# A two-layer decoder trunk on one core: the pooling's channel maps multiplied into the projection's columns on the chip, and a new order of all instructions

## The chip, the core and the metric

The kernel runs on one core of a Trainium2 chip. A core has five engines that each work through a queue of their own in order: TensorE (PE in the profile; matrix products, and PEld for the loading of their stationary operand), VectorE (DVE), ScalarE (ACT), GpSimd (POOL) and SyncE (SP), which issues every DMA of this kernel. Engines wait for each other by semaphores. Data lie in SBUF (128 partitions), matrix products end in PSUM, inputs and stores lie in HBM. The metric is device time of one execution in microseconds (us): 1537.63 us is the median of three runs of the kernel before (1532.89 to 1539.34).

## The reference, cut to what matters

One sequence of 2048 tokens with 1024 channels passes a hybrid layer, a convolution layer and a last RMSNorm, all in float32. The change touches the first projection and the pooling behind it:

```python
def _even_mixer(h, w_in, pool_w, pool_scale, ...):
    proj = jnp.einsum('bsd,de->bse', h, w_in)          # 1024 -> 2048
    u_pool = proj[..., :POOL_WIDTH]                    # 512 channels: 4 groups of 128
    u_ssm = proj[..., POOL_WIDTH:MIX_WIDTH]
    z = proj[..., MIX_WIDTH:]
    y_pool = _multiscale_pool(u_pool, pool_w, pool_scale)
    y_ssm = _s5(u_ssm, ...)                            # diagonal state space model, then a GLU
    y = jnp.concatenate([y_pool, y_ssm], axis=-1) * jax.nn.silu(z)
    return jnp.einsum('bse,ed->bsd', y, w_out)

def _multiscale_pool(u, pool_w, pool_scale):
    ...
    for g, w in enumerate(POOL_WINDOWS):               # windows 2, 4, 8, 16
        c = csum[:, :, g, :]
        lag = jnp.pad(c, ((0, 0), (w, 0), (0, 0)))[:, :s, :]
        outs.append((c - lag) / jnp.minimum(pos, float(w)) - u32[:, :, g, :])
    pooled = jnp.stack(outs, axis=2)
    mixed = jnp.einsum('bsgc,gcd->bsgd', pooled, pool_w)       # one 128x128 map per group
    return mixed.reshape(b, s, POOL_WIDTH) * pool_scale
```

The window mean less the token works along the tokens, channel by channel; the map `pool_w` works along the channels. The second layer is a projection to 3072 columns, a causal convolution over 31 tokens for each of 1024 channels, a LayerNorm, gates and an output projection.

## The kernel before, in words

The tokens are handled as two halves of 1024 (h = 0 and 1, called A and B), each with two blocks of 512 (b). A matrix product of the model is done as three products of rounded operands: every weight and every activation is split by ACT and DVE into a rounded part "hi" (ACT, a CAST, L322) and a rest "lo" (DVE, a subtraction, L290), and `hi*hi + hi*lo + lo*hi` is summed in PSUM (`proj_ops`, products of 128x512, L351). A *unit* is one weight tile of 128 columns against 1024 tokens: 8 x 3 x 2 = 48 such products. For half A the first layer's units stand in the order s0 to s3 (state space columns), then pu0, pz0, pu1, pz1, ... pz3 (pooled columns and their gates), then z0 to z3. The first three units of a half, and the last three of half A, are done block by block, so that three units are open at once. Then come the same units of half B, the output products of A, the second layer of A and so on, at last the output products A.q and B.q.

Everything beside these units is written as small Python generators ("threads") with priorities. `Sched` puts all of it into one order when the program is built: it keeps a clock for each engine, gives each instruction a duration from a formula (in `tt`, `act`, `dma`, `mmb` and others), and takes the instruction that could start first, with a tolerance and the priorities. So the formulas set the order that each engine's queue has on the chip, and nothing else.

Memory is handed out in slots: `mm`, three PSUM tiles of 1024 columns, one for each open unit; `aux`, two PSUM tiles of 512; `raw` (2) for weights as loaded, `w` (8) for their hi and lo; `st` (8), `po` (2), `act` (25) for the rest. `fetch_thread` loads the weights in the units' order, `split_thread` splits them.

The pooling of a half and a group is `pool_thread`: load the projected group (`upd`), add it to shifted copies of itself, subtract the token, load `pool_w`, split both, multiply them in six products into an `mm` tile, load the gate (`z0d`), and multiply PSUM, gate and `pool_scale` on DVE (L308). `x_rates` computes the RMSNorm's factors of a half from eight loads of x; it writes them to HBM with 128x8 single numbers (`rsd`) and loads them back to all partitions. The first evacuation of a unit multiplies by them, so it needs that load. `ssm_prep` and what it spawns compute the tables of the state space model on DVE, ACT and PE and move them by DMA (`Kd`, `Wd`, `Md`).

Of the kernel before, what the change touches and what calls it, by code (L numbers as in the profile page):

```python
# [73 lines left out]
class Sched:  # L74
# [3 lines left out]
    EPS = SLACK  # L78

# [58 lines left out]

    def emit(self, op):
        start = max(self.clk[op.eng], op.ready)  # L140
        if op.eng == "SP":
            issue = start + 0.66
            self.clk["SP"] = issue
            self.dma = max(self.dma, issue) + op.dur
            end = self.dma + 1.9
        else:
            end = start + op.dur
            self.clk[op.eng] = end
# [58 lines left out]

    def run(self):
        while self.threads:
# [13 lines left out]
            est = lambda t: max(self.clk[t.op.eng], t.op.ready)  # L223
            first = min(cand, key=est)
            e0 = est(first)
            eng = first.op.eng
            near = [t for t in cand if t.op.eng == eng and est(t) <= e0 + self.EPS[eng]]
            th = min(near, key=lambda t: (t.bulk, t.prio, est(t)))
# [6 lines left out]
def trunk(ctx, tc, io):  # L235
# [24 lines left out]
    slots("pwt", 1, 256)  # L260
# [24 lines left out]

    def tt(o, a, b, op, eng=None):
        if eng is G:
            return Op("G", 0.25 + width(o) * 2.1e-3, [a, b], [o], lambda: G.tensor_tensor(o, a, b, op))  # L288
        d = 0.13 + width(o) / 960.0 + (0.13 if isps(a, b) else 0.0)
        return Op("V", d, [a, b], [o], lambda: V.tensor_tensor(o, a, b, op))  # L290

    def ts(o, a, s1, s2=None, op0=ALU.mult, op1=None, eng=None):
# [8 lines left out]
        if eng is G:  # L301
            return Op("G", 0.25 + width(o) * 1e-3, rd, [o], emit)
        return Op("V", 0.15 + width(o) / (960.0 if isps(a) else 1920.0), rd, [o], emit)

    def stt(o, a, s, b, op0, op1):
        rd = [a, b] + ([s] if isinstance(s, bass.AP) else [])
        d = 0.13 + width(o) / 960.0 + (0.13 if isps(a, b) else 0.0)
        return Op("V", d, rd, [o], lambda: V.scalar_tensor_tensor(o, a, s, b, op0, op1))  # L308

    def vcopy(o, a):  # L310
        return Op("V", 0.13 + width(o) / 960.0, [a], [o], lambda: V.tensor_copy(o, a))

    def recip(o, a):
        return Op("V", 0.13 + width(o) / 120.0, [a], [o], lambda: V.reciprocal(o, a))

    def scan(o, r, x, ini):
        rd = [r, x] + ([ini] if isinstance(ini, bass.AP) else [])
        return Op("V", 0.13 + width(o) / 480.0, rd, [o], lambda: V.tensor_tensor_scan(
            o, r.to_broadcast([128, width(o)]), x, ini, ALU.mult, ALU.add))

    def acopy(o, a):
        return Op("A", 0.05 + width(o) / 960.0, [a], [o], lambda: A.copy(o, a))  # L322

    def amul(o, a, m):
        return Op("A", 0.1 + width(o) / 960.0, [a], [o], lambda: A.mul(o, a, m))

    def act(o, a, fn, **kw):
# [5 lines left out]
        return Op("A", (0.3 if len(wr) > 1 else 0.13) + width(o) / 960.0, rd, wr, lambda: A.activation(o, a, fn, **kw))  # L333

    def gset(o, v):
        return Op("G", 0.25 + width(o) * 0.5e-3, [], [o], lambda: G.memset(o, v))

    def dma(o, i):
        n = int(np.prod(o.shape)) * 4
        run = 4 * min(a.ap[-1][1] if a.ap[-1][0] == 1 else 1 for a in (o, i))  # L340
        slow = 1.0 if run >= 512 else 1.5 if run >= 256 else 2.0
        return Op("SP", slow * n / 360e3, [i], [o], lambda: SP.dma_start(out=o, in_=i))

    def mmb(batch):

        d = sum(width(o) / 2400.0 if x.dtype == F32R else max(width(o), 128 if w.shape[1] > 64 else 0) / 600.0
                for o, w, x, s, e in batch) + 0.0027 * len(batch)
# [14 lines left out]
    def trb(batch):  # L362
# [3 lines left out]
        op = Op("PE", 0.11 * len(batch), [b[1] for b in batch] + [batch[0][2]], [b[0] for b in batch], emit)  # L366
# [49 lines left out]
    rsd = [dram(f"rsd{h}", (8, 128)) for h in range(2)]  # L416
    Ed = [dram(f"Ed{u}", (128, 1024)) for u in range(8)]
# [11 lines left out]
    class Job:  # L429
        def __init__(self, src, name):  # L430
            self.src, self.name, self.pool = src, name, "w"
# [4 lines left out]
    def job_cols(w, c0, name):  # L436
        return Job(w[c0 // 128], name)

# [76 lines left out]
    def rsqrt_of(o, a, n):  # L515
        t = yield Alloc("sml")
        tv = t[:, :n]
        yield Op("G", 0.3, [a], [o], lambda: G.tensor_tensor(o, a, mhalf[:, :n], ALU.pow))  # L518
# [182 lines left out]

    def pool_worker(h):
# [4 lines left out]
    def pool_thread(h, gi):  # L707
# [16 lines left out]
        if h == 0:  # L724
# [20 lines left out]
        free("st", hi_, lo_)  # L745
        free("pwt", w2)
# [3 lines left out]
        free("st", s)  # L750
# [1055 lines left out]
```

## Time and profile before

| | |
|---|---|
| median of three runs | 1537.63 us |
| the profiled execution | 1537.14 us, its span 1535.3 us |
| mean granted TensorE clock | 0.991 |
| PE busy | 1481.3 us, 96% |
| DVE, ACT, POOL busy | 1128.9, 524.2, 103.6 us |
| DMA | 280.77 MB, mean 183 GB/s |

The profiled execution lies 0.49 us under the median; about 1.8 us of it lie outside the span. PE is busy nearly throughout, so the time is PE's work and the places where PE stands. Busy time of an engine is the union of its instructions: the mean of one product of 128x512 is 397 ns, but they overlap, and one starts every 0.229 us. A product of unrounded float32 operands stands in the trace as two records.

### The profile page before, as it was taken

The numbers are of one execution on the slowest core, as the hardware profiler recorded it, in microseconds if no ns is written. First come the engines' busy times: TensorE is split into PE (matmuls) and PEld (weight loads), VectorE is DVE, ScalarE is ACT, GpSimd is POOL, SyncE is SP. The second block draws the span as 40 slices with busy tenths as digits, with TensorE's granted clock in tenths as the row PEclk, the third lists the DMA queues.
The fourth block names the chain that finished last, engine by engine and source line by source line (L and its number), as shares of the span: only waits on it lengthen the run. The fifth ranks groups of instructions, "written<-read, shape, count | busy, mean of one in ns | idle before, by whom it ended". The sixth has DMA issues, their size and how long they took to land. (4 is left out here: it accounts for less than half of the span.)

```text
span 1535.3 us, 18361 instructions
## 1 busy us (share of the span) xinstructions
PE 1481.3 (96%) x6942; PEld 1213.6 (79%) x6942; DVE 1128.9 (74%) x1318; ACT 524.2 (34%) x829; POOL 103.6 (7%) x313
## 2 busy tenths in 40 slices
PE   5899979999999999999999999999999999999997
PEld 3678768788888888888888888888888888887785
DVE  7882648887877533399999999245997898967652
ACT  6113433122135225311111530352364465443431
POOL 1000010110000002000000000120000000003322
PEclk9999989999999999999999999999999999999999
DMA  8238966877775763223253442623476485956743
GB/s 302 96 97 235 331 193 216 266 239 263 239 252 191 207 229 124 83 83 110 82 111 122 179 164 97 220 83 111 98 177 204 133 284 172 363 206 222 257 158 116
DMA packets 165464, 280.77 MB, mean 183 GB/s; under 512 B 55712, under 2 KB 86144, under 8 KB 165376
## 3 DMA queue, kind: packets, MB, share of 16 engines
q1 hardware_dynamic: 165376, 279.61, 56.1%
q8 instruction: 54, 0.88, 0.2%
q14 instruction: 34, 0.28, 0.1%
HBM read 183.93 MB, written 91.43 MB: 179 GB/s over the span
## 5 line engine op out<-in xcount | busy, mean ns | idle before, releaser
L351 PE MATMUL mm<-act,w 128*128 128x512 f32 x4224 | 1002.3, 397 | 29.0 <-ACT w L322 11.1
L351 PEld LDWEIGHTS mm<-act,w 128*128 128x128 f32 x4224 | 793.1, 189 | 211.8 <-ACT w L322 11.1
L308 DVE SCALAR_TENSOR_TENSOR ca<-cg,cwt,ca 128x1024 f32<-128x1024 f32 (+1 forms) x360 | 397.8, 1106 | 14.5 <-ACT ca L333 4.2
L351 PE MATMUL mm<-w,act 128*128 128x512 f32 x1344 | 318.9, 397 | 1.4 <-DVE w L290 1.4
L351 PEld LDWEIGHTS mm<-w,act 128*128 128x128 f32 x1344 | 253.3, 189 | 60.8 <-DVE w L290 1.9
L322 ACT CAST w<-raw 128x1024 fp32r<-128x1024 f32 (+1 forms) x117 | 121.3, 1038 | 265.8 <-PE mm L351 207.2
L290 DVE TENSOR_TENSOR w<-raw,w 128x1024 fp32r<-128x1024 f32 (+1 forms) x117 | 141.6, 1212 | 51.4 <-ACT w L322 50.1
L333 ACT ACTIVATE junk<-st 128x1024 bf16<-128x1024 f32 (+1 forms) x64 | 54.0, 844 | 135.1 <-DVE st L290 122.3
L290 DVE TENSOR_TENSOR po<-mm,st 128x1024 f32<-128x1024 f32 x32 | 46.6, 1455 | 70.6 <-PE mm L351 65.6
L290 DVE TENSOR_TENSOR st<-st,mm 128x512 f32<-128x512 f32 x48 | 30.9, 684 | 76.0 <-PE mm L351 76.0
L322 ACT COPY st<-aux 128x512 f32<-128x512 f32 (+2 forms) x56 | 25.7, 471 | 129.5 <-PE aux L351 100.8
L322 ACT CAST act<-st 128x512 fp32r<-128x512 f32 (+1 forms) x64 | 51.8, 853 | 46.7 <-DVE st L308 16.6
L333 ACT ACTIVATE act<-act,mask 128x128 f32<-128x128 f32 x192 | 57.8, 390 | 18.8 <-DMA act<-band 18.8
L290 DVE TENSOR_TENSOR act<-st,act 128x512 fp32r<-128x512 f32 (+1 forms) x64 | 56.3, 920 | 3.5 <-ACT act L322 3.3
L308 DVE SCALAR_TENSOR_TENSOR st<-st,mm 128x1024 f32<-128x1024 f32 x24 | 34.4, 1432 | 25.8 <-PE mm L351 25.8
L333 ACT ACTIVATE st<-mm 128x1024 f32<-128x1024 f32 x24 | 24.6, 1026 | 83.2 <-PE mm L351 81.0
L308 DVE SCALAR_TENSOR_TENSOR act<-aux,vcol,act 128x512 fp32r<-128x512 f32 x32 | 22.5, 746 | 40.3 <-ACT act L333 40.3
L518 POOL TENSOR_TENSOR sml<-sml,mhalf 128x1 f32<-128x1 f32 (+2 forms) x38 | 28.0, 736 | 346.5 <-DVE sml L298 343.7
L290 DVE TENSOR_TENSOR st<-st 128x512 f32<-128x512 f32 (+4 forms) x44 | 41.2, 937 | 9.8 <-DMA st<-upd 8.4
L351 PEld LDWEIGHTS aux<-st,act 128*128 128x128 f32 x384 | 45.5, 192 | 2.9 <-ACT act L333 1.4
L351 PE MATMUL aux<-st,act 128*128 128x128 f32 (+1 forms) x384 | 45.5, 274 | 1.1 <-ACT act L333 1.0
L351 PE MATMUL mm<-act,act 128*128 128x512 f32 x192 | 44.9, 393 | 0.8 <-DVE st L290 0.8
(144 smaller groups left out, 937.7 us busy)
## 6 DMA issues: line engine op xcount, KB each, us to landing
raw<-in_odd_w_in SPq DMA_DIRECT2D x48, 512.0 KB, 3.7
raw<-in_even_w_in SPq DMA_DIRECT2D x31, 512.0 KB, 5.1
st<-x1d SPq DMA_DIRECT2D x48, 256.0 KB, 4.9
st<-in_xT SPq DMA_DIRECT2D x16, 512.0 KB, 6.0
st<-in_x SPq DMA_DIRECT2D x16, 512.0 KB, 9.0
raw<-in_even_w_out SPq DMA_DIRECT2D x16, 512.0 KB, 3.7
z1d<-po SPq DMA_DIRECT2D x16, 512.0 KB, 3.2
st<-z1d SPq DMA_DIRECT2D x16, 512.0 KB, 6.2
```

The lines of the kernel that those rows point to most:

```text
L290: return Op("V", d, [a, b], [o], lambda: V.tensor_tensor(o, a, b, op))
L308: return Op("V", d, rd, [o], lambda: V.scalar_tensor_tensor(o, a, s, b, op0, op1))
L322: return Op("A", 0.05 + width(o) / 960.0, [a], [o], lambda: A.copy(o, a))
L333: return Op("A", (0.3 if len(wr) > 1 else 0.13) + width(o) / 960.0, rd, wr, lambda: A.activation(o, a, fn, **kw))
L351: nc.tensor.matmul(o, w, x, start=s, stop=e)
L518: yield Op("G", 0.3, [a], [o], lambda: G.tensor_tensor(o, a, mhalf[:, :n], ALU.pow))
```

## The change

Two things are changed together.

The first is the map of the pooling. The window mean less the token and the channel map can be exchanged, so the map is multiplied into the 512 pooled columns of `even_w_in` instead of onto the pooled sums. The new thread `pool_fold` does it on the chip, once for each of the four groups: it loads the group's columns in a new layout (`pool_in`, with the output channels on the partitions) and the map, multiplies them in 8 float32 products of 128x128 (two times 4 into an `aux` tile), copies the results by ACT and stores them in HBM (`wpd`). The units pu0 to pu3 of both halves load their weights from there (`job_fold`). In `pool_thread` the map's load, the splits of map and sums, the six products and their `mm` tile are gone; the last step multiplies the sums, the gate and `pool_scale` from SBUF.

The second is the order. The formulas for durations are replaced: `dma` now has a duration, an issue time and a landing time by the size of runs, with 8.7 ns for each run under 64 bytes; strided operands, ScalarE's and GpSimd's forms and float32 products have other times; an engine's own earlier write now counts as something to wait for (PE excepted). The whole program is ordered anew by them.

```diff
+    OVER = {"PE": 0.0, "V": 0.084, "A": 0.1, "G": 0.0}
...
-                    if a < hi and lo < b and p0 < q1 and q0 < p1 and (wr or w) and (e != op.eng or e == "SP"):
-                        r = max(r, t + 0.1)
+                    if a < hi and lo < b and p0 < q1 and q0 < p1 and (wr or w) and not (e == op.eng == "PE"):
+                        r = max(r, t + 0.05)
...
         if op.eng == "SP":
-            issue = start + 0.66
-            self.clk["SP"] = issue
-            self.dma = max(self.dma, issue) + op.dur
-            end = self.dma + 1.9
+            dur, issue, land = op.dur
+            self.clk["SP"] = start + issue
+            self.dma = max(self.dma, start + 0.5) + dur
+            end = self.dma + land
...
-        slow = 1.0 if run >= 512 else 1.5 if run >= 256 else 2.0
-        return Op("SP", slow * n / 360e3, [i], [o], lambda: SP.dma_start(out=o, in_=i))
+        rows = n // max(run, 4)
+        if run >= 1024:
+            d = n / 408e3
...
+        else:
+            d = rows * 8.7e-3
...
+    def job_fold(gi, name):
+        return Job(wpd[gi], name, ("wp", gi))
...
+            yield Wait(job.key)
...
+    def pool_fold():
+        yield Wait(("u", "A.s0.0"))
+        for gi in range(4):
+            wt, ot = yield Alloc("st", 2)
+            pw_ = yield Alloc("pwt")
+            yield dma(wt[:, :1024], io["pool_in"][gi])
+            yield dma(pw_, io["pool_w"][0, gi])
+            for q in range(2):
+                ps = yield Alloc("aux")
+                yield mmb([(ps[:, i * 128:(i + 1) * 128], wt[:, (4 * q + i) * 128:(4 * q + i + 1) * 128], pw_,
+                            True, True) for i in range(4)])
+                yield acopy(ot[:, q * 512:(q + 1) * 512], ps)
+                free("aux", ps)
+            free("pwt", pw_)
+            free("st", wt)
+            yield dma(wpd[gi], ot[:, :1024])
+            free("st", ot)
+            done("wp", gi)
...
         free("st", u)
-        w2 = yield Alloc("pwt", None, F32R)
-        pr, = yield Alloc("st", 1)
-        yield dma(pr[:, 0:128], io["pool_w"][0, gi])
-        whi, wlo = w2[:, 0:128], w2[:, 128:256]
-        yield acopy(whi, pr[:, 0:128])
-        yield tt(wlo, pr[:, 0:128], whi, ALU.subtract)
-        free("st", pr)
-        hi_, lo_ = yield Alloc("st", 2, F32R)
-        hi, lo = hi_[:, 0:H], lo_[:, 0:H]
-        yield acopy(hi, s[:, 16:n])
-        yield tt(lo, s[:, 16:n], hi, ALU.subtract)
-        sz = s[:, 0:H]
+        zt = yield Alloc("st")
+        sz = zt[:, 0:H]
         yield Wait(("zp", h, gi))
         yield dma(sz, z0d[h][gi])
-        ps = yield Alloc("mm")
-        yield mmb([(ps[:, b * 512:(b + 1) * 512], w, x[:, b * 512:(b + 1) * 512], i == 0, i == 2)
-                   for i, (w, x) in enumerate(((whi, hi), (whi, lo), (wlo, hi))) for b in range(2)])
...
-        yield stt(sz, ps, vc("pool_scale", gi), sz, ALU.mult, ALU.mult)
-        free("mm", ps)
+        yield stt(sz, s[:, 16:n], vc("pool_scale", gi), sz, ALU.mult, ALU.mult)
...
-            specs.append((f"{p}.pu{gi}", lambda gi=gi: job_cols(w_in0, gi * 128, f"wpu{h}{gi}"), post_pool_u(h, gi)))
+            specs.append((f"{p}.pu{gi}", lambda gi=gi: job_fold(gi, f"wpu{h}{gi}"), post_pool_u(h, gi)))
...
+    spawn(pool_fold(), 3, "fold")
...
+    w["pool_in"] = i["even_w_in"][0][:, :512].reshape(D, 4, 128).transpose(1, 2, 0)
```

Three places show what the new order does.

The head of PE's queue, before: the first unit (s0, tile mm_46) starts at once with its first block; `w_4` is the weight's hi, `w_5` its lo.

```order
L351 MATMUL mm_46_377<-act_1_273,w_4_276 128x512
L351 MATMUL mm_46_377<-act_2_274,w_4_276 128x512
L351 MATMUL mm_46_377<-act_1_273,w_5_277 128x512
L351 MATMUL mm_46_377<-act_1_273,w_4_276 128x512
L351 MATMUL mm_46_377<-act_2_274,w_4_276 128x512
```

The head of PE's queue, now: `st_6` is the first group of `pool_in`, `pwt_8` its map, mm_47 the unit s0.

```order
L390 MATMUL aux_29_318<-pwt_8_284,st_6_282 128x128 x4
L390 MATMUL mm_47_377<-act_1_277,w_4_280 128x512
L390 MATMUL mm_47_377<-act_2_278,w_4_280 128x512
L390 MATMUL mm_47_377<-act_1_277,w_5_281 128x512
L390 MATMUL mm_47_377<-act_1_277,w_4_280 128x512
L390 MATMUL mm_47_377<-act_2_278,w_4_280 128x512
L390 MATMUL mm_47_377<-act_1_277,w_5_281 128x512
L390 MATMUL aux_51_397<-pwt_8_284,st_6_282 128x128 x4
```

Four of the new products have moved ahead of the first unit, four more stand six products into it; the other 24 stand after 84 products of units (4), after 90 (4), after 144 (8), and after 174, behind the first and behind the second group of table products (4 each).

SP's queue around the first write of the RMSNorm's factors, before: `raw` are weights, `po` to `ud` is the store of an evacuated unit.

```order
L342 DMA raw_50_401<-in_even_w_in 128x1024
L342 DMA raw_52_494<-in_even_w_in 128x1024
L342 DMA rsd_189<-sml_26_308 128x8x1
L342 DMA st_55_527<-rsd_189 128x1024
L342 DMA ud_0_117<-po_61_616 128x1024
L342 DMA raw_64_631<-in_even_w_in 128x1024
```

The same place now: `wpd` are the stored folded columns, a `raw` from `wpd` the weights of a pooled unit.

```order
L375 DMA raw_60_502<-wpd_191 128x1024
L375 DMA st_55_430<-in_pool_in 128x1024
L375 DMA pwt_57_432<-in_pool_w 128x128
L375 DMA rsd_189<-sml_28_313 128x8x1
L375 DMA wpd_192<-st_56_431 128x1024
L375 DMA st_73_645<-in_pool_in 128x1024
L375 DMA pwt_75_647<-in_pool_w 128x128
L375 DMA raw_78_668<-in_even_w_in 128x1024
L375 DMA st_67_610<-rsd_189 128x1024
L375 DMA raw_83_710<-wpd_192 128x1024
```

Between the write of the factors and their load stand now a store and a load of the fold and a weight. Further down SP's queue the weights of pu2 have moved from row 34, ahead of the tables' DMAs, to row 72, behind nearly all of them (`Kd`, `Wd`, `Md` and the loads from `Kd`, which now begin at row 44).

PE's queue where half A's last three units are open, before: mm_182 is z2, mm_197 is z3, and the products with `pwt` are the first group's map, into the tile mm_188.

```order
L351 MATMUL mm_188_1754<-st_180_1707,pwt_107_1083 128x512 x2
L351 MATMUL mm_188_1754<-st_181_1708,pwt_107_1083 128x512 x2
L351 MATMUL mm_188_1754<-st_180_1707,pwt_107_1083 128x512 x2
L365 MATMUL aux_192_1768<-ident,act_156_1517 128x128 x4
L351 MATMUL mm_182_1715<-act_6_280,w_162_1559 128x512
L351 MATMUL mm_182_1715<-act_7_281,w_162_1559 128x512
L351 MATMUL mm_182_1715<-act_6_280,w_163_1560 128x512
```

The same place now: mm_233 is z2, mm_235 is z3.

```order
L390 MATMUL mm_233_1973<-act_17_297,w_203_1784 128x512
L390 MATMUL mm_233_1973<-act_18_298,w_203_1784 128x512
L390 MATMUL mm_233_1973<-act_17_297,w_204_1785 128x512
L390 MATMUL mm_235_2008<-act_1_277,w_223_1916 128x512
L390 MATMUL mm_235_2008<-act_2_278,w_223_1916 128x512
```

No tile of the pooling stands any more between the units z1, z2 and z3.

More of the change, by code (lines that the diff above doesn't have):

```diff
@@ L141, in emit @@
         if op.eng == "SP":
-            issue = start + 0.66
-            self.clk["SP"] = issue
-            self.dma = max(self.dma, issue) + op.dur
-            end = self.dma + 1.9
+            dur, issue, land = op.dur
+            self.clk["SP"] = start + issue
+            self.dma = max(self.dma, start + 0.5) + dur
+            end = self.dma + land
         else:
             end = start + op.dur
-            self.clk[op.eng] = end
+            self.clk[op.eng] = end - self.OVER[op.eng]
+            if op.eng == "PE":
+                end += 0.4
         op.emit()
@@ L206, in unblock, with pick @@
         return got[0] if b.n is None else got
+    def pick(self, cand):
+        est = lambda t: max(self.clk[t.op.eng], t.op.ready)
+        first = min(cand, key=est)
+        e0 = est(first)
+        eng = first.op.eng
+        near = [t for t in cand if t.op.eng == eng and est(t) <= e0 + self.EPS[eng]]
+        return min(near, key=lambda t: (t.bulk, t.prio, est(t)))
     def run(self):
@@ L222, in run @@
                     + str({k: len(v) for k, v in self.pools.items()}))
[L223 to L228, printed above, removed]
+            th = self.pick(cand)
             op, th.op = th.op, None
@@ L259, in trunk @@
     slots("sml", 12, 16)
-    slots("pwt", 1, 256)
+    slots("pwt", 1, 128)
     slots("sml2", 1, 64)
@@ L283, in isps, with far, vdur, adur @@
         return any(a.space == bass.MemoryType.PSUM for a in aps)
+    def far(*aps):
+        for a in aps:
+            pat = [p for p in a.ap[1:] if p[1] > 1]
+            if pat and abs(pat[-1][0]) >= 8:
+                return True
+        return False
+    def vdur(c, per, o, *aps):
+        return c + width(o) * per * (1.8 if far(o, *aps) else 1.0)
+    def adur(o, a, n):
+        return (0.18 if isps(a) else 0.2) + 0.09 * n + width(o) * (1.85e-3 if far(o, a) else 0.828e-3)
     def tt(o, a, b, op, eng=None):
         if eng is G:
-            return Op("G", 0.25 + width(o) * 2.1e-3, [a, b], [o], lambda: G.tensor_tensor(o, a, b, op))
-        d = 0.13 + width(o) / 960.0 + (0.13 if isps(a, b) else 0.0)
+            d = 0.35 + 0.2 * width(o) if op == ALU.pow else 0.19 + width(o) * 2e-3
+            return Op("G", d, [a, b], [o], lambda: G.tensor_tensor(o, a, b, op))
+        d = vdur(0.16, 1.035e-3, o, a, b)
         return Op("V", d, [a, b], [o], lambda: V.tensor_tensor(o, a, b, op))
@@ L332, in act @@
             wr.append(kw["accum_out"])
-        return Op("A", (0.3 if len(wr) > 1 else 0.13) + width(o) / 960.0, rd, wr, lambda: A.activation(o, a, fn, **kw))
+        n = sum(isinstance(s, bass.AP) for s in kw.values())
+        return Op("A", adur(o, a, n), rd, wr, lambda: A.activation(o, a, fn, **kw))
     def gset(o, v):
-        return Op("G", 0.25 + width(o) * 0.5e-3, [], [o], lambda: G.memset(o, v))
+        return Op("G", 0.1 + width(o) * 0.8e-3, [], [o], lambda: G.memset(o, v))
     def dma(o, i):
@@ L340, in dma @@
         run = 4 * min(a.ap[-1][1] if a.ap[-1][0] == 1 else 1 for a in (o, i))
-        slow = 1.0 if run >= 512 else 1.5 if run >= 256 else 2.0
-        return Op("SP", slow * n / 360e3, [i], [o], lambda: SP.dma_start(out=o, in_=i))
-    def mmb(batch):
-        d = sum(width(o) / 2400.0 if x.dtype == F32R else max(width(o), 128 if w.shape[1] > 64 else 0) / 600.0
-                for o, w, x, s, e in batch) + 0.0027 * len(batch)
+        rows = n // max(run, 4)
+        if run >= 1024:
+            d = n / 408e3
+        elif run >= 512:
+            d = n / 325e3
+        elif run >= 64:
+            d = rows * (2e-3 if run % 64 and o.space == bass.MemoryType.DRAM else 1.1e-3)
+        else:
+            d = rows * 8.7e-3
+        land = 1.0 if o.space == bass.MemoryType.DRAM else 1.9
+        return Op("SP", (d, 0.42 if rows <= 128 and n > 131072 else 0.6, land), [i], [o],
+                  lambda: SP.dma_start(out=o, in_=i))
+    def mmb(batch):
+        d = 0.0
+        for o, w, x, s, e in batch:
+            if x.dtype == F32R:
+                d += width(o) / 2216.0
+            elif w.shape[1] > 64:
+                d += max(0.224, width(o) * 1e-3)
+            else:
+                d += 0.07 + width(o) * 0.5e-3
         def emit():
@@ L365, in emit @@
                 nc.tensor.transpose(o, a, idn)
-        op = Op("PE", 0.11 * len(batch), [b[1] for b in batch] + [batch[0][2]], [b[0] for b in batch], emit)
+        op = Op("PE", 0.105 * len(batch), [b[1] for b in batch] + [batch[0][2]], [b[0] for b in batch], emit)
         op.n = len(batch)
@@ L416, in trunk @@
     rsd = [dram(f"rsd{h}", (8, 128)) for h in range(2)]
+    wpd = [dram(f"wpd{g}", (128, 1024)) for g in range(4)]
     Ed = [dram(f"Ed{u}", (128, 1024)) for u in range(8)]
@@ L429, in trunk, with __init__ @@
     class Job:
-        def __init__(self, src, name):
-            self.src, self.name, self.pool = src, name, "w"
+        def __init__(self, src, name, key=("go",)):
+            self.src, self.name, self.pool, self.key = src, name, "w", key
         def release(self):
```

23 lines of the change are left out of this document (11 added, 12 removed).

## The prediction

> **What bounds the kernel now.** I read the page's busy shares and slices first, then TensorE's own waits, then the places of those waits in the timeline, then SP's and DVE's queues there.
>
> ```profile
> PE 1481.3 (96%) x6942; PEld 1213.6 (79%) x6942; DVE 1128.9 (74%) x1318; ACT 524.2 (34%) x829; POOL 103.6 (7%) x313
> PE   5899979999999999999999999999999999999997
> 537.60:576.00 38.40, 38.40 (x168) 1.00 0.69 229
> 188.75 0.38 PE L351 MATMUL aux<-act 128*128 128x128 f32 x2
> 190.45 7.87 PE L351 MATMUL mm<-act,w 128*128 128x512 f32 x33
> ```
>
> PE works in every slice but the first, the sixth and the last. The third line is a stretch of 38.4 us in the second layer: 168 products at the full clock, 0.2286 us each; only fewer products or fewer waits shorten that. The last two are the price of a float32 product of 128x128: between these two starts stand 16 records, which are 8 products, in 1.70 us, 0.21 each; I take 0.22.
>
> PE stands for 1535.3 - 1481.3 = 54.0 us. The larger places are these:
>
> ```profile
> 17.77 13.73 PE L351 MATMUL mm<-act,w 128*128 128x512 f32 x48 [5.41 <-DVE w L290]
> 33.82 5.34 PE L351 MATMUL mm<-act,w 128*128 128x512 f32 x22 [2.32 <-DVE w L290]
> 60.16 0.57 PE L351 MATMUL aux<-act,cg 128*32 128x112 f32 x2 [2.09 <-DVE act L290]
> 62.88 0.40 PE L351 MATMUL aux<-act,cg 128*32 128x112 f32 x1 [2.14 <-DVE act L290]
> 64.51 5.68 PE L351 MATMUL mm<-act,w 128*128 128x512 f32 x18
> 168.79 1.16 PE L351 MATMUL aux<-act,st 128*128 128x128 f32 x8 [1.23 <-DMA act<-ud]
> 215.44 37.35 PE L351 MATMUL mm<-act,w 128*128 128x512 f32 x150 [9.61 <-DVE st L308]
> 1408.91 1.10 PE L351 MATMUL aux<-st,onesN 128*128 128x512 f32 x2 [1.36 <-DVE st L290]
> 1438.03 2.83 PE L351 MATMUL mm<-w,act 128*128 128x512 f32 x11 [1.44 <-DVE w L290]
> 1442.68 1.63 PE L351 MATMUL aux<-onesN,st 128*128 128x1 f32 x8 [1.82 <-DVE st L290]
> ```
>
> The number in brackets is the wait just before the row, and what ended it. The largest, 9.61 us, is explained by three queues:
>
> ```profile
> 35.26 0.38 SPq L342 DMA_DIRECT2D rsd<-sml  x1
> 46.33 0.33 SPq L342 DMA_DIRECT2D st<-rsd  x1
> 199.80 0.38 SPq L342 DMA_DIRECT2D rsd<-sml  x1
> 200.22 0.58 SPq L342 DMA_DIRECT2D st<-z0d  x1
> 209.72 0.32 SPq L342 DMA_DIRECT2D st<-rsd  x1
> 214.10 1.28 DVE L308 SCALAR_TENSOR_TENSOR st<-mm,vcol,st 128x1024 f32<-128x1024 f32 x1 [11.40 <-DMA st<-z0d]
> ```
>
> Each write of the factors (`rsd`, 1024 single numbers) holds its load back for 11.07 and 9.92 us. The pooling's gate load (`z0d`) went out 0.42 us behind the second one, so DVE's last pooling step waited 11.40 us. That step frees the map's `mm` tile, and PE needed a third tile for z3.
>
> **The change, part by part.** The sum is made against the profiled execution, 1537.14 us, which is 0.5 us under the median.
>
> *PE's work.* Gone are the map's 48 products, 6 for each half and group: 48 x 0.2286 = 11.0 us. Added are 32 float32 products, 32 x 0.22 = 7.0 us. Net -4.0; between -2.5 and -5.5 if a new product costs 0.27 (the mean of one row, overlap and all) or 0.18.
>
> ```profile
> L351 PE MATMUL mm<-st,pwt 128*128 128x512 f32 x48 | 12.6, 397 | 0.0
> L290 DVE TENSOR_TENSOR st<-st,st 128x1024 fp32r<-128x1024 f32 x8 | 9.8, 1223 | 0.7 <-ACT st L322 0.7
> L322 ACT CAST st<-st 128x1024 fp32r<-128x1024 f32 x8 | 8.4, 1045 | 0.0
> ```
>
> *DVE, ACT and DMA off the path.* DVE loses the 9.8 us of the second row and 8 small subtractions, ACT the 8.4 us of the third and 8 small casts, SP eight loads of 64 KB. ACT gains 8 copies of a half `aux`, SP 4 loads of 64 KB and 4 loads and 4 stores of 512 KB. I cost these at nothing: away from the places above PE is the engine that others wait for. Without that cover DVE's gain would be at most its 9.8 us.
>
> *The head.* The first four new products need the first group of `pool_in`, row 10 of SP's queue; ahead of it lie six loads of x and two weights, 4.2 MB, with it 4.74 MB.
>
> ```profile
> 0.00:4.00 4.00, 0.00 (x0) 1.00 0.45 127
> 4.00:8.00 4.00, 0.00 (x0) 1.00 1.00 373
> 8.00:12.00 4.00, 0.87 (x2) 1.00 1.00 399
> 12.00:16.00 4.00, 0.35 (x1) 1.00 1.02 412
> ```
>
> The last column is GB/s: 0.51, 1.49, 1.60 and 1.65 MB make 5.2 MB by 16 us, so the data come at about 15 to 16 us. Before, PE got through two products and then waited for the weight's lo until 17.77 us. Now four fold products run in that time. -0.9 (they cost no path), between -1.5 and +3 if the load lands 3 us later, since every unit stands behind it in PE's queue.
>
> *The wait at 33.8 us.* The third weight's lo stood behind 12 steps of the tables in DVE's queue; now it stands ahead of them, and its load is 1 MB further ahead, so that it lands near 26 us.
>
> ```profile
> L333 ACT ACTIVATE junk<-st 128x1024 bf16<-128x1024 f32 x32 | 33.8, 1057 | 46.0 <-DVE st L290 33.7 <-DMA st<-in_x 11.3
> ```
>
> ACT has four such squares of x ahead of its cast, from about 23.8 us on; with the cast and DVE's subtraction I get the lo at 31 us, and PE, at 0.2286 us a product behind the head, at 31.5: -1.8, between -2.3 and +1.
>
> *The tables (57.8 to 64.5 us).* DVE stood for 4.99 us before the first evacuation because it waited for the factors; table steps that PE wanted stood behind that.
>
> ```profile
> 50.58 2.27 DVE L290 TENSOR_TENSOR po<-mm,st 128x1024 f32<-128x1024 f32 x1 [4.99 <-DMA st<-rsd]
> 60.00:66.00 6.00, 3.69 (x32) 0.54 0.47 152
> ```
>
> Now those steps stand ahead of the evacuation. The two waits of 2.09 and 2.14 go, with three of 0.46 to 0.56 behind them: 5.8. The clock stood at 0.54 in this stretch: the 18 products at 64.51 took 5.68 us instead of 18 x 0.2286 = 4.1, another 1.5. Together -7.3. What is late next: s3 needs an `mm` tile, so an evacuation, so the factors. Their write goes out at about 39.5 us instead of 35.3 (1.7 MB of fold and one more weight now lie ahead of the last x, at the 410 GB/s above), its load 11 us later, and behind a fold store, a fold load and a weight, 1.6 MB or 4 us. The evacuation ends at about 60 us. PE has its 144 products, 24 folds and the waits above behind it at 57.4. New wait +3.0, between 0 and +6.
>
> By the Trainium skill, page "TensorE: Matmul & The Clock Gate", section "What's actually happening", the clock halves after an idle window of about 3.4 us and needs as long a busy one to come back. The two waits of 2.1 us with 0.57 us of work between them, each below that, did halve it here. By the page's window the new single wait of 3 us would cost no clock and the sum stays; by these rows it could cost another 1.5.
>
> *The wait at 215 us.* The pooling has no `mm` tile any more, so z3 can start; and the gate's load now stands 33 rows ahead of the second `rsd`. -9.6. The clock came back late:
>
> ```profile
> 212.00:216.00 4.00, 0.56 (x1) 0.50 0.94 361
> 216.00:220.00 4.00, 4.00 (x11) 0.50 0.95 318
> 220.00:224.00 4.00, 4.00 (x17) 0.88 0.58 235
> ```
>
> From 215.44 to 224 there is room for 37 products and 29 were done: 8 x 0.2286 = 1.9. Together -11.5; -4 if another evacuation is held by a late DMA there.
>
> *The end.* The LayerNorm of half B's second block stood in PE's queue until 48 products into B.q; now it stands 180 products into A.q, over 200 earlier, so DVE does not split B.q's weights and the LayerNorm at once. The three waits (4.6) can go, and the slow clock behind them:
>
> ```profile
> 1444.00:1448.00 4.00, 4.00 (x11) 0.50 0.89 245
> 1448.00:1452.00 4.00, 4.00 (x15) 0.78 1.02 376
> ```
>
> 26 products where 35 have room, 9 x 0.2286 = 2.1. Gain 6.7. But now two LayerNorms stand close together, and their products were put as close behind DVE as before; I keep two waits of the size of the one at 1408.91, 2 x 1.4 = 2.8. Net -3.9, between -6.7 and +3.
>
> *The rest.* The wait at 168.79 and its like (1.23, and eight of 1 us or less, 5.0 in all) I keep: the same chains stand there.
>
> Sum: -4.0 - 0.9 - 1.8 - 7.3 + 3.0 - 11.5 - 3.9 = -26.4, so 1537.1 - 26.4 = 1510.7, rounded 1511 us.
>
> **Rivals.**
>
> *Slower: pu2 starves behind the tables' DMAs.* Its weights stand behind 64 issues of SP.
>
> ```profile
> 106.67 3.87 SPq L342 DMA_DIRECT2D rsc<-act  x6
> 137.66 1.07 SPq L342 DMA_DIRECT2D raw<-in_even_w_in  x2
> 158.00 2.81 SPq L342 DMA_DIRECT2D st<-Kd  x4
> raw<-in_even_w_in SPq DMA_DIRECT2D x31, 512.0 KB, 5.1
> ```
>
> From 110.6 to 137.66 us stand 41 issues, 0.66 us each. The first table products stand 30 unit products behind s3's start at 60 us; so SP can reach the tables' DMAs at 70 us, and then pu2's load goes out at 70 + 64 x 0.66 = 112. PE has 384 products, the fold and the tables behind it at about 125; landing (5.1), cast and subtraction (2.3) ask for an issue by 117. A margin of 5 us, and from there PE loses a us for each. If the tables run as late as before, when their last load was issued at 160.8, PE stands 44 us: 1511 + 44 = 1555. Against it: before, SP stood behind the units' stores until 106 us, and those now stand behind the tables.
>
> *Half is given back.* The rest of the order is new too; if the margin above goes by 5 us and LayerNorm and state space products wait as often again as in the profile before (6.2 us, and the 1.8 at the end that I took off), 1511 + 13 = 1524.
>
> *No change.* Were the wait at 215 only moved, as an evacuation behind the second `rsd` (9.6 + 1.9), and the head 10 us late behind the fold, it would be 1533. For it speaks that PE waits in order; against it the rows moved.
>
> *All goes well.* No new wait at s3, none at the LayerNorms: 1511 - 3 - 2.8 = 1505, with the head's and the fold's better ends 1503.
>
> **How the numbers follow.** Forecast (1505 to 1518) 0.5, half given back (1518 to 1529) 0.2, all well (1497 to 1505) 0.12, no change 0.1, starved 0.08. Half a per cent, 7.7 us, is about what a measurement tells: faster means under 1530. Faster 0.82, same 0.1, slower 0.08. From 1499 to 1529 lie the first two cases and most of the third, 0.8.
>
> **What would show it.** In the profile after: no row of products with `pwt` as the stationary operand's map into `mm`, 64 records from `pool_in`; PE's first row at 15 to 17 us; a wait of some 3 us near 57 us that ends with DVE's `po`; none above 3 us at 200 to 220 us; LayerNorm products before the middle of A.q. I am wrong if PE waits over 5 us for a DMA of weights at 110 to 130 us, or if the waits after 330 us, hardly any now, sum to over 10.

## The result, and the profile after

The changed kernel takes 1546.68 us (median of 4 runs, 1546.02 to 1548.53); the kernel before took 1535.37 us beside it (1532.89 to 1539.34). The ratio is 1.0073, 95% interval 1.005 to 1.0097: slower by 11 us where 26 us less were forecast. The profiled execution has a span of 1544.6 us.

The page of the changed kernel: busy time of PE, and its busy tenths and clock in 40 slices of 38.6 us.

```profile
span 1544.6 us, 18374 instructions
PE 1481.6 (96%) x6958; PEld 1213.8 (79%) x6958; DVE 1112.2 (72%) x1302; ACT 516.6 (33%) x821; POOL 94.6 (6%) x313
PE   5898998999999999999999999999999999899997
PEclk9998999999999999999999999999999999999999
```

PE stands for 1544.6 - 1481.6 = 63.0 us (54.0 before), and its busy time has not fallen, although its work has: some of it ran at a lower clock. The places where the prediction saw waits, in PE's timeline of the changed kernel:

```profile
15.74 2.05 PE L390 MATMUL aux<-pwt,st 128*128 128x128 f32 x8 [15.74 <-DMA pwt<-in_pool_w]
60.00 2.07 PE L390 MATMUL aux<-pwt,st 128*128 128x128 f32 x8 [3.04 <-ACT st L344]
211.94 40.44 PE L390 MATMUL mm<-act,w 128*128 128x512 f32 x174
```

The first is the head, where it was forecast; the second is the one new wait that was; the third runs through z3 without the 9.61 us of before. These are new:

```profile
132.18 2.05 PE L390 MATMUL aux<-act,st 128*128 128x128 f32 x8 [6.83 <-DMA act<-ud]
182.75 2.05 PE L390 MATMUL aux<-act,st 128*128 128x128 f32 x8 [3.62 <-DMA act<-ud]
256.74 2.08 PE L390 MATMUL aux<-act,st 128*128 128x128 f32 x8 [4.36 <-DMA act<-ud]
1341.45 1.10 PE L390 MATMUL aux<-st,onesN 128*128 128x512 f32 x2 [2.15 <-DVE st L312]
1353.58 2.05 PE L390 MATMUL aux<-st,onesN 128*128 128x512 f32 x2 [4.10 <-DVE st L312]
```

The first three are the first products of state-space units, which wait for the load of their input (`ud`, `load_u`, 256 KB). The other two are the means of the last two LayerNorms. PE's waits by group, of the whole kernel:

```profile
PE aux L390 <- DMA act<-ud: 15.2, 5, 6.8
PE aux L390 <- DVE st L312: 9.3, 4, 4.1
PE mm L390 <- DVE w L312: 3.8, 3, 2.1
```

(us in all, times, longest.) Before, the first of these was:

```profile
PE aux L351 <- DMA act<-ud: 2.1, 3, 1.2
```

To see where the time went I compare the start of the same product of 128x512 in both traces, the pooling's map left out. At the 2017th product, in A's first output products, when all state-space work is done, the changed kernel is 3.5 us *ahead* (578.4 against 581.9 us); at the last of 5760 it is 8.9 us behind. So the first part gave 3.5 us where 22.5 were forecast, and the second lost 12.4 where 3.9 were to be gained. I call them the first and the second part below. The profiled execution of the kernel before (1537.14 us) lies 3 to 4 us over the medians of that kernel beside the experiments (1532.8 to 1534.3), so distances from it, here and below, flatter the other kernel by about as much.

### The profile page after: what moved, and what is told of

It reads as the page before. It is cut to its first block, busy times and chain, and to the rows that moved or that the text cites. A ratio compares the mean times of both kernels' runs of the same rounds, so it can differ in the third digit from the quotient of the medians.

```text
span 1544.6 us, 18374 instructions
## 1 busy us (share of the span) xinstructions
PE 1481.6 (96%) x6958; PEld 1213.8 (79%) x6958; DVE 1112.2 (72%) x1302; ACT 516.6 (33%) x821; POOL 94.6 (6%) x313
## 5 line engine op out<-in xcount | busy, mean ns | idle before, releaser
L344 ACT COPY st<-aux 128x512 f32<-128x512 f32 (+2 forms) x64 | 30.1, 484 | 127.6 <-PE aux L390 103.4
L312 DVE TENSOR_TENSOR st<-st 128x512 f32<-128x512 f32 (+4 forms) x44 | 40.8, 934 | 15.7 <-DMA st<-upd 15.2
L330 DVE SCALAR_TENSOR_TENSOR act<-aux,vcol,act 128x512 fp32r<-128x512 f32 x32 | 22.5, 746 | 40.5 <-ACT act L356 40.5
```

The source lines that it names most:

```text
L344: return Op("A", adur(o, a, 0), [a], [o], lambda: A.copy(o, a))
```

## Why the first state-space load was late

SP's timeline of the changed kernel, the tables' DMAs and what stands behind them:

```profile
87.92 4.64 SPq L375 DMA_DIRECT2D st<-Kd  x7
111.54 0.59 SPq L375 DMA_DIRECT2D raw<-wpd  x1
114.52 4.30 SPq L375 DMA_DIRECT2D act<-act  x4
118.91 2.01 SPq L375 DMA_DIRECT2D Md<-st  x1
120.98 1.20 SPq L375 DMA_DIRECT2D st<-upd  x1
122.28 1.03 SPq L375 DMA_DIRECT2D raw<-wpd  x1
124.35 0.85 SPq L375 DMA_DIRECT2D act<-ud  x1
```

SP issues without a pause. The load of pu2's weights (`wpd`) goes out at 111.54 us, as the prediction's slow rival worked it out (112), and PE does not wait for it. But 13 rows behind it stands the state-space input's load, and these rows take 12.8 us, about 1 us each: loads and stores of 256 to 520 KB, for which the table has 0.42 us. Worked out with the table's own prices, the load was to be issued at 111.2 us, to land at 117.5, and its products to start at 118.55. On the chip the issue was 13.1 us later, PE came to the place 6.8 us later (at 125.35), and nearly all of the rest is the wait. Most of the 13.1 us is older than these rows: in the plan they take 10.4 us too, since SP stands twice there for data. The first store of `Kd` (at 73.14 us) was already 6.2 us behind the plan; the 58 rows from there to pu2's load took 0.66 us each where the plan has 0.58, another 4.5; the 13 rows added the last 2.4. What the wait did to the clock, in windows of 4 us (length, PE busy with its records, granted clock, DMA share, GB/s):

```profile
124.00:128.00 4.00, 1.34 (x6) 1.00 1.00 314
128.00:132.00 4.00, 0.00 (x0) 0.51 1.05 397
132.00:136.00 4.00, 3.82 (x13) 0.50 1.05 417
136.00:140.00 4.00, 4.00 (x14) 0.71 0.70 243
```

The DMA engines are full and the clock halves; in the last two rows 27 records (the first 8 of them of only 128x128) stand where 35 products of 128x512 have room.

In the second part DVE stands first, and PE behind it:

```profile
1338.88 0.52 SPq L375 DMA_DIRECT2D act<-cd  x1
1345.41 1.23 DVE L312 TENSOR_TENSOR st<-act,act 128x1024 f32<-128x1024 f32 x1 [2.96 <-DMA act<-cd]
1346.55 1.22 DVE L312 TENSOR_TENSOR ca<-ca,aux 128x1024 f32<-128x1024 f32 x1
1352.75 0.68 DVE L312 TENSOR_TENSOR st<-st 128x512 f32<-128x512 f32 x1
```

The last of a LayerNorm's four loads of 512 KB goes out at 1338.88 us; DVE waits for loads of this group until 1345.41, sums, and ends at 1353.43; between its sums stand three steps of 1.2 us like the third row, which use the mean of the LayerNorm ahead. PE's mean product starts then, 4.10 us after PE came to it. Two LayerNorms stand 30 products apart (240 before).

## Experiments

Every ratio below is to the kernel before, run beside it on the same chip, with its 95% interval. The kernel before had medians from 1532.8 to 1535.4 us on the different chips, so differences between medians of different rounds are good to some 3 us; where it matters the difference of the ratios stands beside them. "Price" is the number by which the planner reckons, not what the chip needs.

**Which half of the change: e1 and e2.** Theory A blames the new durations, theory B the fold. e1 is the kernel before with only the fold's lines of the diff, e2 with only the durations'.

```diff
 e1, against the kernel before: the fold, old durations
+    spawn(pool_fold(), 3, "fold")
-        ps = yield Alloc("mm")
...
 e2, against the kernel before: durations, no fold
-        d = sum(width(o) / 2400.0 if x.dtype == F32R else max(...) / 600.0
-                for o, w, x, s, e in batch) + 0.0027 * len(batch)
+            if x.dtype == F32R:
+                d += width(o) / 2216.0
...
```

> The fold alone, planned with the old durations. Its order keeps the state-space products' first batch at product 510 (372 in the changed kernel) and the last LayerNorm at product 5298 (5028). Theory A, the new durations are at fault (they put products ahead of loads that SP issues late): no wait over 3 us for the state-space input load, 4.0 us of product work gone and the wait of 9.6 us at 215 us gone, so 1515 to 1530 us, about 1521. Theory B, the fold is at fault (its loads and stores of 512 KB hold up SP's queue in the first 130 us): 1540 us or more, with waits for DMAs before 140 us.

> The new durations alone, with the maps multiplied onto the sums as before. Its order puts the state-space products at 396 and the last LayerNorm at 5076, about as early as the changed kernel does. Theory A: the waits for the state-space input load stand here too, over 8 us in all, and the LayerNorms' waits in the second layer, so 1542 to 1556 us. Theory B: no such wait without the fold's DMAs; the table waits at 58 to 64 us and the one at 215 us are gone, 1520 to 1532 us.

The fold alone: 1525.53 us, 0.9949 (0.9931 to 0.9967). The durations alone: 1547.12 us, 1.0089 (1.0074 to 1.0105). The loss is the durations'. As theory A had it, the durations alone bring the waits of the changed kernel back almost as they were. One detail differs from it: the fold alone still waits for a state-space load, up to 8.4 us at once. PE's waits, e1 and then e2:

```profile
PE aux L351 <- DMA act<-ud: 11.7, 4, 8.4
```

```profile
PE aux L390 <- DMA act<-ud: 17.3, 5, 7.9
PE aux L390 <- DVE st L312: 8.7, 4, 3.7
```

**The two places: e3 and e4.** Each is the changed kernel with one row held back.

```diff
 e3
+HOLD = {0: 'A.pz2', 1: 'A.pu3', 2: 'A.pz3', 3: 'A.z0', 4: 'B.s0.1', 5: 'B.s2.1'}
...
+            if u in HOLD:
+                yield Wait(("u", HOLD[u]))
             yield from ssm_unit(0, u, UM, GT, EE, WW)
 e4
-    spawn(ln_thread(1, 1, y1[1]), RANK["lnb"], "lnB1")
+    spawn(after(("u", "A.q.e0t2"), ln_thread(1, 1, y1[1])), RANK["lnb"], "lnB1")
```

> The changed kernel, only that the first six batches of state-space products are held back in TensorE's order by 42 to 84 products (432 instead of 372, and so on); loads and everything else are planned as in the changed kernel. Theory A: the waits of 6.8, 3.6 and 4.4 us for the state-space input load fall to under 1 us each, and the half clock behind them goes too; 1526 to 1534 us. Rival, SP's queue is late for everything: the same time is stood elsewhere before 300 us (weights, the x of half B), 1543 to 1550 us.

> The changed kernel, only that the LayerNorm of half B's second block starts 60 to 90 products later (its mean's products at 5118 instead of 5028). Theory A (two LayerNorms too close behind each other on DVE): the waits of 2.2 and 4.1 us at 1341 and 1354 us go, 1538 to 1542 us. Rival (DVE stands for the conv results' loads wherever the products are put): the same waits stand some 20 us later, 1545 to 1549 us.

e3: 1535.36 us, 1.002 (1.0009 to 1.0032), 11 us under the changed kernel (8 by the ratios) and 1.4 us over theory A's range. At the 2017th product it is 12.0 us ahead of before (changed kernel 3.5). Its waits:

```profile
PE aux L391 <- DMA act<-ud: 3.6, 3, 1.5
PE aux L391 <- DVE st L313: 8.0, 4, 3.9
```

So the place of these products made 8.5 of the 19.0 us that the first part lacks against the forecast. The second part loses 8.7 us (12.4 in the changed kernel) by nearly the same waits (second row). New in the first part are waits of transposes near the held rows for DVE, one at 137 us of 2.80 us.

e4: 1548.15 us, 1.011 (1.008 to 1.014), nothing gained, as the rival had it. The waits only moved; behind 1180 us they are 13.6 us in all (13.9 in the changed kernel), among them:

```profile
PE aux L390 <- DVE st L312: 6.6, 5, 2.0
PE mm L390 <- ACT w L344: 1.2, 1, 1.2
```

(The held LayerNorm had stood at 4998 and not, as I wrote, at 5028; the other one moved from there to 5052, so that they now stand 66 apart.) So it is not the closeness of the two alone; in both orders DVE ends a little behind PE. That led to theory C: both places lose because the planner puts each row where its data are *just* there, and the old table's price for a product of 128x512, 0.2160 us, was too low. (0.2286 us is measured; the new price is 0.2310.) With it PE came later than planned to everything that another engine or a DMA hands over.

**One number: e5 to e8.**

```diff
 e5, against the changed kernel
-                d += width(o) / 2216.0
+                d += width(o) / 2400.0 + 0.0027
 e6, against e1
-        d = sum(width(o) / 2400.0 if x.dtype == F32R else ...
+        d = sum(width(o) / 2216.0 - 0.0027 if x.dtype == F32R else ...
 e7, against the changed kernel
-        land = 1.0 if o.space == bass.MemoryType.DRAM else 1.9
-        return Op("SP", (d, 0.42 if rows <= 128 and n > 131072 else 0.6, land), ...
+        land = 2.4 if o.space == bass.MemoryType.DRAM else 4.0
+        return Op("SP", (d, 0.42 if rows <= 128 and n > 131072 else 0.66, land), ...
 e8: the edits of e3 and e5 together
```

> The changed kernel with one number of the table put back: the planner takes 0.2160 us for a product of 128x512, as before the change, instead of 0.2310 (0.2286 was measured). The order that comes out has the first state-space products at 396 (372), the last LayerNorm's at 5250 (5028). Theory C, the too low price was the slack: TensorE came later than planned at everything, so loads and DVE were in time; with the true price each error of the other prices is a wait. By C the waits behind 1190 us fall from 13.9 us to under 7, those for the state-space input load from 15.2 to under 9, and the kernel takes 1528 to 1539 us. Rival, only the DMA prices count: no change, 1543 to 1549 us.

> The fold alone with the old durations but for one number: 0.2310 us for a product of 128x512 instead of 0.2160. Its order has the state-space products at 522 (510 without the edit) and the last two LayerNorms' at 5016 and 5058 (5058 and 5298). Theory C: the waits behind 1190 us, 5.4 us in the fold alone, rise to over 10, and the kernel loses 4 to 12 us against the fold alone: 1529 to 1538 us. Rival, only the DMA prices count: 1522 to 1528 us, as the fold alone.

> The changed kernel with two prices of DMAs raised towards what its trace shows: 0.66 us for an issue of a small DMA (0.60), and 4.0 us until a load (1.9) and 2.4 us until a store (1.0) counts as landed behind the queue's own end. The state-space products come out at 408 (372), the last LayerNorms' at 5052 and 5232 (4998 and 5028). If the planned landing is what was too early: the waits for the state-space input load fall from 15.2 to under 7 us, those behind 1190 us from 13.9 to under 10; 1530 to 1539 us. If the product's price alone counts: 1543 to 1549 us.

> Both cures at once: the state-space products held back as in the run before (e3) and the product's price put back to 0.2160 us as in e5. If the two losses lie in different places they add up: about 10 us from the state space, 6 to 9 us from the second layer, so 1524 to 1531 us. If both cures only move the same waits, no better than the better one of them alone, 1533 to 1537 us.

e5: 1513.78 us, 0.9868 (0.985 to 0.9885), 33 us under the changed kernel by one number; theory C had expected 8 to 19. Its page and its waits:

```profile
span 1512.1 us, 18364 instructions
PE 1470.1 (97%) x6958; PEld 1209.8 (80%) x6958; DVE 1112.9 (74%) x1302; ACT 517.9 (34%) x821; POOL 100.5 (7%) x313
PE aux L390 <- DMA act<-ud: 4.9, 2, 4.1
PE aux L390 <- DVE st L312: 2.5, 3, 1.8
```

PE has the same 6958 records as in the changed kernel. The spans differ by 32.5 us: PE stands 21.0 us less (42.0 against 63.0) and is busy 11.5 us less (mean granted clock 0.995 against 0.988). I had counted the waits and not the clock behind them.

e6, the converse: 1553.29 us, 1.0128 (1.011 to 1.0145), 28 us slower than e1. The direction is theory C's; the size is again over twice its range, and the waits do not sit where it put them (7.8 us behind 1180 us where over 10 were expected). They are spread over the whole kernel, and PE is busy 11.1 us longer than in e1.

e7: 1531.49 us, 0.9987 (0.9977 to 0.9998). Dearer DMAs cure most of the first part (15.2 us ahead of before at the 2017th product) and little of the second (9.0 us lost against 12.4; its waits are 12.7 us where under 10 were expected):

```profile
PE aux L390 <- DMA act<-ud: 2.7, 2, 2.3
PE mm L390 <- DVE w L312: 4.9, 1, 4.9
```

So the DMAs' prices are a cause of the first part's loss too, but hardly of the second's. e8: 1511.26 us, 0.9863 (0.9846 to 0.988), the lowest median here. Beside e5 the hold brings 2.5 us, which is within the intervals, and not the 10 that I had added up: in the first part the two cures take away the same waits. So far the rival was right, though the time is below both ranges, as e5's was. What is left of the waits:

```profile
PE aux L391 <- DMA act<-ud: 0.5, 1, 0.5
PE aux L391 <- DVE st L313: 1.5, 2, 0.8
```

**How far it goes: e9 to e12.** e9 and e10 have `width(o) / 2292.0` and `width(o) / 2500.0` in e5's place.

```diff
 e11, against the changed kernel
-                        r = max(r, t + 0.05)
+                        r = max(r, t + (1.5 if op.eng == "PE" else 0.05))
 e12, against e2
-                d += width(o) / 2216.0
+                d += width(o) / 2400.0 + 0.0027
```

> The changed kernel with a price of 0.2234 us for a product of 128x512, half way between the changed kernel's 0.2310 and the 0.2160 of e5 (measured 0.2286). Theory C (the slack between planned and real time is what counts): between the two, 1520 to 1540 us, with waits for the state-space input load between 5 and 15 us. Rival, the order falls out better or worse by accident with every edit: anything between 1505 and 1555 us, without a trend.

> The changed kernel with a price of 0.2048 us for a product, twice as far below the measured 0.2286 as e5's. Theory C: the remaining waits for state-space loads behind 100 us (4.9 us in e5) go, nothing else is gained, and rows that are now put later cost at the end at most what they gain: 1506 to 1516 us. Rival, accident: outside of that.

> The changed kernel with its true product price of 0.2310 us, but the planner counts what another engine or a DMA hands to TensorE as ready 1.5 us later (0.05 us). State-space products come out at 372 as before this edit, the last LayerNorms' at 5022 and 5160 (4998 and 5028). If a fixed margin does what the low price does: 1515 to 1530 us. If the lag must grow with the distance (SP's queue was late by 10 us and more when the first state-space load was issued): the wait at 132 us stays over 5 us, the waits behind 1190 us fall below 8, and 1530 to 1542 us.

> No fold (the maps multiplied onto the sums as before the change), with the new durations and the price of 0.2160 us of e5. The state-space products come out at 438 (396 with the true price), the last LayerNorms' at 5082 and 5298. Theory C: 1512 to 1524 us, and what e5 is faster than this is the worth of the fold, 4 us of product work by my sum. Rival, the low price only helps where the fold's DMAs stand in SP's queue: above 1535 us.

e9: 1534.96 us, 1.0004 (0.999 to 1.0017), between its neighbours as expected. e10: 1534.67 us, 1.0006 (0.9995 to 1.0017), a miss: 21 us slower than e5. At the 2017th product it is as far ahead as e5 (18.3 against 20.7 us); it loses in the second part, as the rival (accident) would have it. Its waits there:

```profile
PE aux L404 <- ACT st L356: 6.6, 4, 2.6
PE aux L390 <- DVE st L312: 6.0, 1, 6.0
```

The first are the transposes of the next activations, at 982 and 1013 us, the second a LayerNorm's variance at 1357 us. Why these rows come late stays open. e11: 1549.58 us, 1.0113 (1.0094 to 1.0133), a miss of both ranges: the wait at the first state-space load stays (8.0 us), as the second view had it, and beside what is left of the LayerNorms' waits (4.7 us) others come behind 1180 us:

```profile
PE mm L390 <- DVE act L312: 8.6, 4, 6.8
PE mm L390 <- ACT act L344: 6.8, 3, 2.6
```

But the two parts differ. In its profiled execution, the fastest of five, e11 is 16.6 us ahead of before at the 2017th product, nearly as far as with the low price, and loses 22.8 from there. So a fixed 1.5 us at each hand-over buys most of the first part, with the longest wait still in it, and does harm in the second; that the low price works as slack there too is not shown by it. e12, without the fold: 1534.35 us, 1.0006 (0.9995 to 1.0017), 10 us over theory C's upper end, so the fold is worth some 20.6 us at the low price, five times its products; at the changed kernel's price it is worth next to nothing (1.0089 for e2, 1.0073 with the fold), and with the old durations 7.3 us (e1). e12 is 1.2 us ahead at the 2017th product where e5 is 20.7; its waits are again for DVE and ACT around 218 to 260 us, where the pooling with its splits now runs. Which of the fold's effects that is stays open.

**Slack or accident: e13 to e16.** e13 has the price of 0.2160 us only from the second layer's first unit on, e14 only up to it; e15 and e16 take 0.2140 and 0.2290 us.

```diff
 e13, against the changed kernel
-                d += width(o) / 2216.0
+                d += width(o) / 2400.0 + 0.0027 if ("u", "A.g0.0") in sc.keys else width(o) / 2216.0
```

> The changed kernel with the price of 0.2160 us only from the second layer's first unit on; the first layer's order is that of the changed kernel (state-space products at 372), the second's that of e5 (last LayerNorm's at 5250). If the losses are local and add up: against the changed kernel the part behind product 2016 gains what e5 gained there, 15 us, and the first layer nothing: 1529 to 1535 us. If the order is an accident as a whole: no such sum, under 1525 or over 1540.

> The changed kernel with the price of 0.2160 us only up to the second layer's first unit; the first layer's order is that of e5 (state-space products at 396), the second's that of the changed kernel (last LayerNorm's at 5028). If the losses are local and add up: the first layer gains what e5 gained there, 17 us, and the second stays slow: 1526 to 1533 us. If not: under 1520 or over 1538.

> A near neighbour of e5: a price of 0.2140 us. By slack: 1508 to 1522 us, and no row of the second layer waits over 3 us. By accident of the order: a difference of over 10 us from e5's 1513.8.

> The price that is measured, 0.2290 us, nearly the changed kernel's 0.2310. By slack: 1537 to 1550 us, with over 12 us of waits for the state-space input load. By accident of the order: under 1530.

e13: 1532.66 us, 1.0002 (0.999 to 1.0013). e14: 1526.80 us, 0.9962 (0.9948 to 0.9976). Against the changed kernel that is -14.0 and -19.9 us, together -33.9; both at once (e5) give -32.9. (By the ratios 0.71 and 1.11%, together 1.82%, and 2.05%.) The losses are local and add up. The waits, e13 and then e14:

```profile
PE aux L390 <- DMA act<-ud: 16.7, 4, 7.1
PE aux L390 <- DVE st L312: 1.3, 2, 0.7
```

```profile
PE aux L390 <- DVE st L312: 8.6, 5, 3.0
PE aux L390 <- DMA act<-ud: 4.6, 5, 3.2
```

e15: 1512.60 us, 0.9868 (0.9855 to 0.9881), as e5. e16: 1543.36 us, 1.0072 (1.006 to 1.0085), as the changed kernel. All in one table; the two last columns are the profiled execution's distance from the profiled execution before, at the 2017th product and from there to the last (minus is ahead, in us):

| kernel | price of a product | median | first part | second part |
|---|---|---|---|---|
| changed | 0.2310 | 1546.68 | -3.5 | +12.4 |
| e16 | 0.2290 | 1543.36 | -3.8 | +12.8 |
| e9 | 0.2234 | 1534.96 | -9.9 | +8.2 |
| e5 | 0.2160 | 1513.78 | -20.7 | -2.6 |
| e15 | 0.2140 | 1512.60 | -17.1 | -5.0 |
| e10 | 0.2048 | 1534.67 | -18.3 | +16.2 |
| e13 | 0.2310, then 0.2160 | 1532.66 | -4.6 | -1.2 |
| e14 | 0.2160, then 0.2310 | 1526.80 | -19.4 | +8.7 |
| e3 | 0.2310, held rows | 1535.36 | -12.0 | +8.7 |
| e7 | 0.2310, dearer DMAs | 1531.49 | -15.2 | +9.0 |
| e11 | 0.2310, 1.5 us of margin | 1549.58 | -16.6 | +22.8 |
| e8 | 0.2160, held rows | 1511.26 | -22.2 | -3.8 |

From 0.2310 down to 0.2160 both parts gain steadily. Below that the first part stays and the second breaks somewhere between 0.2140 and 0.2048. Between near neighbours a part differs by up to 4 us (e5, e15; and in the second part the changed kernel, e3 and e14, whose last LayerNorms stand at the same products): that much is the accident of an order or of an execution. For the first part, four different edits that put rows later (the low price, the hold, dearer DMAs, the margin) all gain, from 8.5 to 17.2 us. For the second only the price does; that it does so as slack is argued from the waits that go, and not shown by itself.

## Why the prediction was wrong, point by point

- *The waits that go.* Right in kind: those at 33.8 us, around the tables and at 215 us are gone. At the 301st product, where both kernels have the same table products behind them and the changed one all of the fold, it is 1.4 us ahead (107.55 against 108.95 us); the forecast's terms up to there (7.0 for the fold, -0.9, -1.8, -7.3, +3.0) sum to 0.0. The whole loss lies behind it. The new wait ahead of s3 was forecast at 3.0 us near 57 us and came at 3.04 us, but that match is luck: the row waits for ACT's copy of a fold product, and ACT had stood for a weight; the factors, on which the forecast rested, held DVE at the same time, and its first evacuation, which frees s3's tile, ended at 61.33 us, just ahead of s3's start at 61.72.

```profile
58.41 1.04 ACT L344 CAST w<-raw 128x1024 fp32r<-128x1024 f32 x1 [7.16 <-DMA raw<-in_even_w_in]
59.31 3.97 DVE L312 TENSOR_TENSOR po<-mm,st 128x1024 f32<-128x1024 f32 x2 [3.96 <-DMA st<-rsd]
```

  The wait did cost clock:

```profile
60.00:64.00 4.00, 4.00 (x15) 0.59 0.46 179
1340.00:1344.00 4.00, 2.55 (x10) 1.00 1.04 384
```

  Fifteen records stand there; the second row holds the single wait of 2.15 us, behind which the clock stayed whole. The Trainium skill's page "TensorE: Matmul & The Clock Gate", section "What's actually happening", has the clock halve after an idle window of about 3.4 us. The waits of 6.83 and 2.15 us agree with that; the 3.04 us do not by themselves, with 1.13 us of work and a wait of 1.21 us ahead of them.
- *PE's work.* Start to start, as the forecast counted, four of the fold's products took 0.80 or 0.81 us in three groups, 0.20 each (0.22 assumed). Two of the eight groups took 1.70 and 1.72 us, in the head and at the clock of 0.59, some 1.8 us more in all. (Their busy time, 10.7 us, counts overlaps and compares with the 12.6 us of the map's products.)
- *The head.* 15.74 us, inside 15 to 17. (In the term for the wait at 33.8 us, PE at 31.5 instead of 33.82 us is a gain of 2.3 and not of 1.8; that changes little.)
- *"The rest ... I keep: the same chains stand there."* This is the step that failed. The chains were the same, their places were not: the first state-space products had moved from product 546 to 372, and the term was 5.0 us for all of them. The waits for `ud` alone came to 15.2 us, and the clock behind them was lost as well. I had followed this very queue for the rival "pu2 starves", got its issue right within 0.5 us, and did not go 13 rows further, to the next load that PE waits for. e3 shows what that was worth: 8.5 us in the first part. SP reached that load 13.1 us later than the plan had it and PE 6.8 us later.
- *"The end: -3.9."* Wrong in sign. The rows in PE's and DVE's queues moved as described, and I argued from one effect (the LayerNorm no longer meets the splits of B.q's weights). The LayerNorms' sums moved just as far ahead and now waited for the loads of the convolution's results. The bound of +3 for this term was too near; it was +12.4 for the whole second part. The prediction's own sign of being wrong, waits over 10 us behind 330 us, came true.
- *What both have in common* I had not asked: what the new durations do to the slack, the time by which PE comes later to a row than the plan has it. I took them for a better order and looked for what they repair. The old price of a product was 5.5% under the measured 0.2286 us; e5 and e6 show that this error carried the kernel. By e14 the first part with the low price is 19.4 us ahead of before, which is near my 22.5, so gains of that size were there to be had; that each of my terms has its share in it is not shown.

## What to carry to other kernels

Where a plan sets the order, prices that are nearer to the truth can make a kernel slower: an order that leaves no slack turns errors of the other prices into waits of the bounding engine. Try pricing that engine a few per cent under what it needs (here 0.2160 or 0.2140 served for 0.2286, and 0.2048 was too much), at several values, since the time has a minimum and not a trend. Dearer DMAs helped less than half as much here, and a fixed margin not at all. And when an order changes, list for every load that the bounding engine waits for how many rows it moved; a queue that is nearly late for one can be late for the next behind it, as SP was here 13 rows on.

## What was unexpected of the hardware

- SP's issues are not of one length: some 0.66 us each for the tables' small DMAs from 84 to 111 us (42 issues in 27.7 us), and about 1 us for the 13 behind them, up to 2.01 us, while the DMA share rose from 0.85 (112 to 116 us) to 1.03 (116 to 124; 0.67 to 0.89 in the stretch ahead). Loads of 256 KB of `ud` landed 6.4 us after their issue in the median of 16 (3.0 to 7.9).
- A wait costs more than its length: between the changed kernel and e5, 11.5 us of busy time for the same 6958 records went with 21.0 us of waiting.
